# Encoder trunk on one core: rotary tables built beside the projections, vector loads on another queue, a two-part sum of squares, and a drawn order in the mixer's opening

## The chip, the cores and the metric

The kernel runs on one core of a Trainium2 chip. The metric is the device time of one execution in microseconds (us). The engines of the core run side by side: PE (TensorE, matmuls), DVE (VectorE), ACT (ScalarE), POOL (GpSimd) and SP (SyncE, here only a queue that issues transfers). Each engine takes its instructions in the order in which the program lists them; an instruction whose operand is not ready holds up everything behind it on its engine. A DMA can be issued from the queue of SP or of ACT.

## What is computed

Two layers of an encoder over 1024 tokens of width 1024. Cut to what matters here:

```python
cos, sin = rope_tables(positions)              # 1024 x 16 each
c_act = silu(c)
for l in range(2):
    mod = c_act @ w_ada[l] + b_ada[l]          # shift, scale, gate for both sub-layers
    h = rmsnorm(x, g_mix[l]) * (1 + scale_a) + shift_a
    proj = h @ w_in[l]                         # q,k,v of the neighbourhood branch, c_q, c_kv, k_rope, gates
    # latent branch: q = rmsnorm(c_q) @ w_uq; its rotary part is turned by cos, sin
    ...                                        # two attention branches, gates, merge
    x = x + gate_a * (merged @ w_out[l])
    h = rmsnorm(x, g_mlp[l]) * (1 + scale_m) + shift_m
    x = x + gate_m * (square(relu(h @ w_ff1[l])) @ w_ff2[l])
return rmsnorm(x, g_final)
```

## The kernel before

A scheduler puts the instructions of all engines into one order when the kernel is built; `keep_in_program_order` (called `pin`) keeps an instruction at its place among the pinned ones. Activations lie transposed, 128 channels by 512 tokens to a tile, two halves of the tokens (`ch` 0 and 1). Every fp32 operand of a matmul is split into a high part (a cast on ACT, L201) and a low part (a subtraction on DVE, L202), and a product is three matmuls, high by high, high by low and low by high (L208 to L210, or L459 to L461). So each operand costs ACT and DVE one instruction before PE can use it. Below, "h lo" and "wq lo" are such subtractions for the activations and the weights.

**The opening.** SP's queue issues the loads of `c`, the positions, eight rows `xrow` of x (512 KB each), seven small vectors (`vrows`, L116), and then 16 tiles `wada` of 512 KB with the adaLN weights for the first scale and the first shift. DVE first builds the rotary tables: the angles of all positions, in turns, reduced to their fraction by exact pieces (L302 to L325), from which ACT computes `sinT` and `cosT` by Sin (L350, L351) with a load of the Sin table before and of the Exp/Ln table behind. ACT squares the rows of x (L337), POOL makes of each sum a reciprocal root and a diagonal matrix `dg` (L338 to L342), and PE multiplies xrow by it into `pyT`, which transposes and scales in one step. DVE adds up the `wada` tiles with the weights `c_act`, one row each (L169, then L171): eight for the scale, eight for the shift. PE turns the sums (`pada`), DVE reduces them (`mod`), and with them the normed x becomes h.

**The projections** (`projections`, L449). Eight units of `ptok` (24 matmuls each) give `ctok`, that is c_q, c_kv and k_rope for 128 tokens each; `c_sink` copies and scales them on DVE, `cg`, `cqh` and `cql` are their transposed high and low parts. Eight units with the weights `ws` of `vws` give `vtok`. Beside these `query_rot` turns c_q into rotary queries: PE `pqr`, DVE `rot` and `qrr` (L386 to L392, which read sinT and cosT), and two units later `query_turn` transposes them (`pqrT`, L756). A further eight wada tiles are added up here for the next vector of the modulation.

**The norm before the mixer and the final ones.** `square_sum` squares each of eight channel tiles on ACT and adds it to `sums` on DVE; `rstd_first` multiplies `sums` by a matrix of ones in fp32 on PE (`pss`), which gives every partition the sum over channels; DVE takes `var` from it. This happens six times in a run: for both halves before each of the two mixers, and for both halves before layer 1's projections.

**The mixer's opening** (`mixer_norm_rest` and `mixer`). The mixer multiplies by Winograd's form of Strassen's scheme: seven products p = 1..7 for each step i, of sums of blocks of h and of the weights. In what follows (i,p) is such a product, 12 matmuls of 128x512. `norm` is a generator that, in steps between the first products, scales the second half of h and makes the sums `operand_h(p, k, ...)`; `weight_operands` makes the sums `s` of the weights. The order of the products is written out, the order of the DVE and ACT work below them is the scheduler's.

Of the kernel before, what the change touches and what calls it, by code (L numbers as in the profile page):

```python
# [18 lines left out]
P = 128  # L19
# [18 lines left out]
def hybrid_trunk(  # L38
# [89 lines left out]
    nc.sync.dma_start(pint, positions.rearrange("a (i p) -> (a i) p", p=P))  # L128
# [71 lines left out]
    def split(dst_hi, dst_lo, src, pin=lambda ins: ins):  # L200
        pin(A.copy(dst_hi, src))  # L201
        V.tensor_tensor(dst_lo, src, dst_hi.bitcast(F32), op=ALU.subtract)  # L202
# [28 lines left out]
    sums = [None, None]  # L231

    def square_sum(src, ch, n):
# [64 lines left out]
    n, chunks, magic = P, turn_chunks(), 1.5 * 2.0 ** 23  # L298
    turns, rest = (pool["ws"].tile([P, 2048], F32, tag="ws", name=s) for s in ("turns", "rest"))
    ang, parts = rest[:, 1792:1920], rest[:, 1536:1792]  # L300
    for i in range(8):
        V.tensor_scalar(ang[:, i * 16:(i + 1) * 16], invf, posT[:, i:i + 1], None, op0=ALU.mult)  # L302
    ahi = parts[:, n:]
    V.tensor_copy(ahi.bitcast(F32R), ang)
    V.tensor_tensor(parts[:, :n], ang, ahi, op=ALU.subtract)

    def frac(t):
        w = rest[:, :t.shape[1]]
        V.tensor_scalar(w, t, magic, magic, op0=ALU.add, op1=ALU.subtract)
        V.tensor_tensor(t, t, w, op=ALU.subtract)  # L310

    m = 2 * n * len(chunks)
    for i, cval in enumerate(chunks):
        V.tensor_scalar(turns[:, 2 * n * i:2 * n * (i + 1)], parts, cval, None, op0=ALU.mult)
    frac(turns[:, :m])
    frac(turns[:, :m])
    while m > n:
        half = m // n // 2 * n
        V.tensor_tensor(turns[:, :half], turns[:, :half], turns[:, m - half:m], op=ALU.add)
        frac(turns[:, :half])  # L320
        m -= half
    two_pi = 2.0 * math.pi * (1 - 2.0 ** -22)
    flat = lambda t: t[:].rearrange("p a b -> p (a b)")
    turn, quarter = turns[:, :n], turns[:, n:2 * n]
    V.tensor_scalar(quarter, turn, 0.25, None, op0=ALU.add)  # L325
    frac(quarter)
# [1219 lines left out]
```

## Time and profile before

| | |
|---|---|
| median of 3 runs | 3153.73 us (3151.32 to 3154.35) |
| the profiled execution | 3154.83 us, its span 3153.0 us |
| mean granted clock of PE | 0.988 |
| PE busy | 3033.6 us, 96% |
| DVE / ACT / POOL busy | 66% / 47% / 12% |

PE is nearly always busy, so what counts is the time in which it waits, and what it is waiting for. A busy share of the other engines is an average over stages of very different kinds. The profiled execution lies 1.10 us above the median.

### The profile page before, as it was taken

The numbers are of one execution on the slowest core, as the hardware profiler recorded it, in microseconds if no ns is written. First come the engines' busy times: TensorE is split into PE (matmuls) and PEld (weight loads), VectorE is DVE, ScalarE is ACT, GpSimd is POOL, SyncE is SP. The second block draws the span as 40 slices with busy tenths as digits, with TensorE's granted clock in tenths as the row PEclk, the third lists the DMA queues.
The fourth block names the chain that finished last, engine by engine and source line by source line (L and its number), as shares of the span: only waits on it lengthen the run. The fifth ranks groups of instructions, "written<-read, shape, count | busy, mean of one in ns | idle before, by whom it ended". The sixth has DMA issues, their size and how long they took to land. (4 is left out here: it accounts for less than half of the span.)

```text
span 3153.0 us, 43333 instructions
## 1 busy us (share of the span) xinstructions
PE 3033.6 (96%) x15104; PEld 2456.0 (78%) x15104; DVE 2069.4 (66%) x3911; ACT 1471.2 (47%) x2820; POOL 373.0 (12%) x518
## 2 busy tenths in 40 slices
PE   7999999999998999999989999999999999999998
PEld 6878886776786888888777788777777778888887
DVE  8534436767859776877774334466775697767775
ACT  6234446554127666433352444555522466663332
POOL 5111002232200000000011011123221000000000
PEclk9999999999999999999999999999999999999999
DMA  6554334214853656856334444431266255586652
GB/s 258 157 135 111 99 109 119 63 36 145 280 191 107 244 207 231 293 196 209 106 121 138 125 121 114 117 86 36 73 214 218 69 180 214 211 308 205 215 166 84
DMA packets 359540, 497.56 MB, mean 158 GB/s; under 512 B 30556, under 2 KB 238618, under 8 KB 359322
## 3 DMA queue, kind: packets, MB, share of 16 engines
q1 hardware_dynamic: 359322, 494.80, 48.9%
q8 instruction: 119, 1.95, 0.3%
q14 instruction: 99, 0.81, 0.1%
HBM read 335.41 MB, written 141.98 MB: 151 GB/s over the span
## 5 line engine op out<-in xcount | busy, mean ns | idle before, releaser
L208 PE MATMUL pd<-h,wh 128*128 128x512 f32 x768 | 307.0, 400 | 0.6 <-ACT wh L201 0.6
L210 PE MATMUL pd<-h,wh 128*128 128x512 f32 x768 | 300.7, 392 | 0.0
L209 PE MATMUL pd<-h,wh 128*128 128x512 f32 x768 | 300.1, 391 | 0.0
L208 PE MATMUL pxz<-ho,wq 128*128 128x512 f32 x672 | 259.9, 392 | 3.5 <-DVE xT L1401 3.0
L209 PE MATMUL pxz<-ho,wq 128*128 128x512 f32 x672 | 261.8, 390 | 0.5 <-DVE ho L1153 0.5
L210 PE MATMUL pxz<-ho,wq 128*128 128x512 f32 x672 | 257.0, 389 | 0.0
L201 ACT CAST wq<-s 128x512 fp32r<-128x512 f32 (+3 forms) x296 | 154.5, 541 | 125.5 <-PE pxz L210 54.2
L208 PE MATMUL px<-h,wq 128*128 128x512 f32 x512 | 202.2, 396 | 3.5 <-ACT u L1242 2.3
L1401 DVE SCALAR_TENSOR_TENSOR xT<-pxz,mod,xT 128x512 f32<-128x512 f32 x252 | 186.7, 744 | 28.4 <-PE pxz L210 28.3
L798 DVE TENSOR_REDUCE sm<-smla 128x1 f32<-128x1024 f32 x128 | 156.6, 1223 | 69.7 <-PE smla L796 63.3
L209 PE MATMUL px<-h,wq 128*128 128x512 f32 x512 | 200.2, 392 | 1.4 <-DVE h L202 1.4
L210 PE MATMUL px<-h,wq 128*128 128x512 f32 x512 | 199.6, 391 | 0.0
L801 ACT ACTIVATE pmla<-smla,sm 128x1024 f32<-128x1024 f32 x128 | 143.0, 1117 | 118.2 <-DVE sm L799 113.3
L803 POOL TENSOR_SCALAR pmla<-pmla,sm 128x1024 f32<-128x1024 f32 x128 | 144.6, 1130 | 330.4 <-DVE sm L799 153.7
L202 DVE TENSOR_TENSOR wq<-s,wq 128x512 fp32r<-128x512 f32 (+3 forms) x296 | 168.7, 582 | 6.9 <-ACT wq L201 6.9
L796 PE MATMUL smla<-st,st 128*128 128x512 f32 x512 | 170.4, 413 | 2.9 <-ACT pmla L801 2.9
L208 PEld LDWEIGHTS pd<-h,wh 128*128 128x128 f32 x768 | 144.9, 189 | 32.4 <-issue 3.4
L210 PEld LDWEIGHTS pd<-h,wh 128*128 128x128 f32 x768 | 144.6, 188 | 32.8 <-issue 1.0
L209 PEld LDWEIGHTS pd<-h,wh 128*128 128x128 f32 x768 | 145.1, 189 | 28.3
L201 ACT CAST wq<-wr 128x384 fp32r<-128x384 f32 (+3 forms) x218 | 114.7, 539 | 106.2 <-PE pxz L210 62.6
L209 PE MATMUL pyz<-h,wq 128*128 128x512 f32 x384 | 151.6, 395 | 8.0 <-DVE h L202 8.0
L208 PEld LDWEIGHTS pxz<-ho,wq 128*128 128x128 f32 x672 | 126.1, 188 | 36.3 <-issue 4.8
(281 smaller groups left out, 7344.3 us busy)
## 6 DMA issues: line engine op xcount, KB each, us to landing
hid_d<-diff SPq DMA_DIRECT2D x112, 512.0 KB
ho<-hid_d SPq DMA_DIRECT2D x112, 512.0 KB
wada<-in_w_ada_dram SPq DMA_DIRECT2D x96, 512.0 KB
wr<-in_w_ff_dram SPq DMA_DIRECT2D x64, 512.0 KB
w<-in_w_in_dram SPq DMA_DIRECT2D x56, 512.0 KB
wr<-in_w_ff_dram SPq DMA_DIRECT2D x64, 384.0 KB
ho<-hid_d SPq DMA_DIRECT2D x84, 256.0 KB
hid_d<-u SPq DMA_DIRECT2D x68, 256.0 KB
```

The costliest lines, as they stand in the source:

```text
L201: pin(A.copy(dst_hi, src))
L202: V.tensor_tensor(dst_lo, src, dst_hi.bitcast(F32), op=ALU.subtract)
L208: T.matmul(ps, wh, mh, start=first and i == 0, stop=False, **kw)
L209: T.matmul(ps, wh, ml, start=False, stop=False, **kw)
L210: T.matmul(ps, wl, mh, start=False, stop=i == n - 1, **kw)
L796: T.matmul(ps[:, cs(ch)], a[:, t], b[:, cs(ch)], start=i == 0, stop=i == 2)
L798: V.reduce_max(sm[:, 0:1], ps, axis=AX.X)
L801: A.activation(pt, ps, AF.Exp, bias=sm[:, 1:2], scale=MLA_SCALE, accum_out=sm[:, 2:3])
L803: G.tensor_scalar(pt, pt, sm[:, 3:4], 1.0, op0=ALU.mult, op1=ALU.mult)
L1401: V.scalar_tensor_tensor(x, ps, gate_m[:, nt:nt + 1], x, op0=ALU.mult, op1=ALU.add)
```

## The change

Four edits. (1) The rotary tables are no longer built ahead of the opening's adaLN sums; `rotary_tables` is called from `c_sink` with the fifth unit of `ptok` in layer 0, works in three slabs instead of two weight tiles, and pins its first eight rows and its two Sins. (2) The nine loads of vectors and positions are issued from ACT's queue instead of SP's. (3) The last of the eight squares is no longer added to `sums` on DVE; a second fp32 matmul with ones adds it on PE, in the same bank. (4) In the mixer's opening `follow` makes instructions follow others on the same engine: the scaling of tile k = 4 of the second half follows the last `operand_h(5, 3)`, and the weight sums of the work items 8 to 11 follow its DVE part.

```diff
 def load_rows(group, base):
-            nc.sync.dma_start(t[n:n + cnt, :], flat.rearrange("(r p) -> r p", p=P))
+            nc.scalar.dma_start(t[n:n + cnt, :], flat.rearrange("(r p) -> r p", p=P))
...
-    nc.sync.dma_start(pint, positions.rearrange("a (i p) -> (a i) p", p=P))
+    nc.scalar.dma_start(pint, positions.rearrange("a (i p) -> (a i) p", p=P))
...
+    def follow(ins, prev):
+        tc.add_manual_dep(ins.ins, prev.ins.name, mybir.DependencyInfo(mybir.DependencyClass.NoSync, mybir.DependencyReason.DATA),
+                          reason="order of the mixer's opening")
+        return ins
...
             sq = tmp("sq")
             A.activation(sq, src, AF.Square)
-            V.tensor_tensor(sums[ch], sums[ch], sq, op=ALU.add)
+            if n < 7:
+                V.tensor_tensor(sums[ch], sums[ch], sq, op=ALU.add)
+            else:
+                last_sq[ch] = sq
...
-        T.matmul(ps, ones, sums[ch], start=True, stop=True)
+        T.matmul(ps, ones, sums[ch], start=True, stop=False)
+        T.matmul(ps, ones, last_sq[ch], start=False, stop=True)
...
+    def rotary_tables():
+        n, chunks, magic = P, turn_chunks(), 1.5 * 2.0 ** 23
+        ta, tb, tw = (slab(s) for s in ("turns", "turns", "rest"))
...
+        pin(A.activation(flat(sinT), turn, AF.Sin, scale=two_pi))
+        pin(A.activation(flat(cosT), quarter, AF.Sin, scale=two_pi))
+        exp_ln_tables()
...
+            if i == 4 and l == 0:
+                rotary_tables()
...
+                v = V.tensor_tensor(y, y, r, op=ALU.mult)
+                a = A.activation(y, y, AF.Identity, scale=amlp[l][:, k:k + 1], bias=shift_m[:, k:k + 1])
+                if k == 4 and ch == 1:
+                    follow(a, opening[0])
+                    follow(v, opening[1])
...
-                operand_h(5, k, top[k][0])
+                opening[:] = operand_h(5, k, top[k][0])
...
+            ins = V.tensor_tensor(t, x0, x1, op=op)
+            if wait_opening[0]:
+                follow(ins, wait_opening[0])
...
+            wait_opening[0] = opening[1] if 8 <= n < 12 else None
```

What this does to the order of the engines is shown at three places. SP's queue at the start of the program, before (xrow is a row of x, vrows the small vectors, wada the adaLN weights):

```order
L132 DMA xrow_98<-in_x_dram 128x1024
L132 DMA xrow_100<-in_x_dram 128x1024
L116 DMA vrows_102<-in_b_ada_dram 96x128
L116 DMA vrows_102<-in_g_mix_dram 16x128
L116 DMA vrows_105<-in_g_mlp_dram 16x128
L116 DMA vrows_105<-in_g_final_dram 8x128
L116 DMA vrows_105<-in_b_gate_dram 32x128
L116 DMA vrows_105<-in_g_q_dram 4x128
L116 DMA vrows_105<-in_g_kv_dram 2x128
L160 DMA wada_201<-in_w_ada_dram 128x1024
L160 DMA wada_203<-in_w_ada_dram 128x1024
```

The same place on SP's queue in the change:

```order
L132 DMA xrow_98<-in_x_dram 128x1024
L132 DMA xrow_100<-in_x_dram 128x1024
L160 DMA wada_164<-in_w_ada_dram 128x1024
L160 DMA wada_166<-in_w_ada_dram 128x1024
L160 DMA wada_168<-in_w_ada_dram 128x1024
```

The loads of wada stand directly behind those of x; the two loads that stood ahead of x have gone too, and all nine now head ACT's queue, before its first table load.

DVE beside the first units of the projections, before, up to the first rotary rows (`rot`, `qrr`), which are rows 147 and 148 of DVE's order:

```order
L169 TENSOR_SCALAR ada_1563<-wada_1564,c_act 128x1024
L171 SCALAR_TENSOR_TENSOR ada_1563<-wada_1567,c_act,ada_1563 128x1024
L664 TENSOR_SCALAR cg_1062<-pcT_1058,cols 128x128 x3
L171 SCALAR_TENSOR_TENSOR ada_1563<-wada_1570,c_act,ada_1563 128x1024
L202 TENSOR_TENSOR cql_725<-cg_1062,cqh_724 128x128
L202 TENSOR_TENSOR cql_727<-cg_1062,cqh_726 128x128
L202 TENSOR_TENSOR cql_729<-cg_1062,cqh_728 128x128
L664 TENSOR_SCALAR cg_1106<-pcT_1102,cols 128x128 x3
L171 SCALAR_TENSOR_TENSOR ada_1563<-wada_1573,c_act,ada_1563 128x1024
L386 TENSOR_TENSOR rot_1125<-pqr_1117,sinT 128x128
L387 TENSOR_TENSOR qrr_1124<-pqr_1117,cosT 128x8x16
```

DVE ahead of the same rotary rows in the change, where they are rows 157 and 159 (turns and rest are the tables in the making):

```order
L171 SCALAR_TENSOR_TENSOR ada_1568<-wada_1587,c_act,ada_1568 128x1024
L321 TENSOR_SCALAR rest_804<-turns_802 128x384
L171 SCALAR_TENSOR_TENSOR ada_1568<-wada_1590,c_act,ada_1568 128x1024
L322 TENSOR_TENSOR turns_802<-turns_802,rest_804 128x384
L334 TENSOR_TENSOR turns_802<-turns_802 128x128
L321 TENSOR_SCALAR rest_804<-turns_802 128x128
L322 TENSOR_TENSOR turns_802<-turns_802,rest_804 128x128
L339 TENSOR_SCALAR turns_802<-turns_802 128x128
L402 TENSOR_TENSOR rot_1130<-pqr_1122,sinT 128x128
L322 TENSOR_TENSOR turns_802<-turns_802,rest_804 128x128
L403 TENSOR_TENSOR qrr_1129<-pqr_1122,cosT 128x8x16
```

Four of the eight wada rows (three L171 and the L169) stood ahead of the first `rot` before, and all eight do now, with the rows of the tables between them. PE's order of units is unchanged here: `pqr` for two tiles, the second unit of vtok, `pqrT` twice, `pqr`, the third unit.

DVE in the mixer's opening of layer 0, before (u<-pyz are rows on finished products, xT the scaling and the sums of h; h_8669 is the low part of the first operand of p = 5, wq_8758 that of the weights of (0,3)):

```order
L1284 TENSOR_TENSOR u_8694<-pyz_8781,u_8694 128x512
L1162 TENSOR_TENSOR s_8800<-wr_8633,s_8798 128x512
L1162 TENSOR_TENSOR s_8884<-wr_8624 128x512
L202 TENSOR_TENSOR wq_8758<-s_8756,wq_8758 128x512
L1162 TENSOR_TENSOR s_8923<-wr_8631 128x512
L1284 TENSOR_TENSOR u_8722<-pyz_8833,u_8722 128x512
L1077 TENSOR_TENSOR xT_7947<-xT_7951,xT_7947 128x512
L1077 TENSOR_TENSOR xT_7948<-xT_7952,xT_7948 128x512
L202 TENSOR_TENSOR h_8669<-xT_7947,h_8669 128x512
```

DVE around the same operand in the change (numbers of tiles are five higher):

```order
L1063 TENSOR_TENSOR xT_7959<-xT_7959,r_1505_8618 128x512
L202 TENSOR_TENSOR wq_8731<-s_8729,wq_8731 128x512
L1088 TENSOR_TENSOR xT_7952<-xT_7952 128x512
L1088 TENSOR_TENSOR xT_7953<-xT_7953 128x512
L1088 TENSOR_TENSOR xT_7954<-xT_7954 128x512
L1311 TENSOR_TENSOR u_8699<-pyz_8786,u_8699 128x512
L1088 TENSOR_TENSOR xT_7955<-xT_7955 128x512
L1311 TENSOR_TENSOR u_8727<-pyz_8838,u_8727 128x512
L1100 TENSOR_TENSOR xT_7953<-xT_7957,xT_7953 128x512
L202 TENSOR_TENSOR h_8674<-xT_7952,h_8674 128x512
```

Counted from `var`, the row behind pss, h_8669 was the 37th row of DVE and is the 27th as h_8674; the low part of the weights of (0,3), which was the 32nd, is the 46th as wq_8763. Layer 1 has the same rows in both orders, but for wq of (0,3), which was the 62nd there.

## Rows read from the trace of the kernel before

**Rows 1.** The page, busy time and share of the span by engine.
```profile
PE 3033.6 (96%) x15104; PEld 2456.0 (78%) x15104; DVE 2069.4 (66%) x3911; ACT 1471.2 (47%) x2820; POOL 373.0 (12%) x518
```
**Rows 2.** Waits of PE: line, waited for, us in all, times, longest.
```profile
PE pyT L347 <- POOL dg L342: 11.1, 5, 6.4
```
**Rows 3.** Timeline of SP's queue: start us, us, rows issued.
```profile
1.51 3.76 SPq L132 DMA_DIRECT2D xrow<-in_x_dram  x8
...
15.14 13.95 SPq L160 DMA_DIRECT2D wada<-in_w_ada_dram  x16
```
**Rows 4.** Timeline of DVE in the opening: start, us, rows, idle before.
```profile
13.71 0.62 DVE L309 TENSOR_SCALAR rest<-turns 128x768 f32<-128x768 f32 x1
14.36 0.96 DVE L310 TENSOR_TENSOR turns<-turns,rest 128x768 f32<-128x768 f32 x1
...
19.71 0.75 DVE L169 TENSOR_SCALAR ada<-wada,c_act 128x1024 f32<-128x1024 f32 x1
...
38.08 1.28 DVE L187 TENSOR_REDUCE mod<-pada 128x4 f32<-128x512 f32 x2
...
42.08 3.92 DVE L171 SCALAR_TENSOR_TENSOR ada<-wada,c_act,ada 128x1024 f32<-128x1024 f32 x3
```
**Rows 5.** Timeline of PE in the opening.
```profile
28.05 8.37 PE L347 MATMUL pyT<-dg,xrow 128*128 128x128 f32 x58 [2.15 <-POOL dg L342]
...
55.19 0.45 PE L459 MATMUL ptok<-ws,h 128*128 128x416 f32 x1
```
**Rows 6.** Timeline of POOL in the opening.
```profile
8.18 1.90 POOL L342 TENSOR_SCALAR dg<-ident,xss 128x128 f32<-128x128 f32 x1
```
**Rows 7.** Timeline of DVE beside the projections.
```profile
84.18 1.22 DVE L202 TENSOR_TENSOR ws<-w,ws 128x1024 fp32r<-128x1024 f32 x1
...
110.62 1.27 DVE L171 SCALAR_TENSOR_TENSOR ada<-wada,c_act,ada 128x1024 f32<-128x1024 f32 x1
111.82 0.28 DVE L386 TENSOR_TENSOR rot<-pqr,sinT 128x128 f32<-128x128 f32 x1
```
**Rows 8.** Timeline of PE at the first rotary queries.
```profile
117.89 0.66 PE L756 MATMUL pqrT<-ident,qrr 128*128 128x128 f32 x2 [1.87 <-DVE qrr L392]
```
**Rows 9.** Timeline of PE at three of the six sums of squares.
```profile
933.32 1.02 PE L245 MATMUL pss<-sums,ones 128*128 128x512 f32 x2
...
953.36 1.59 PE L245 MATMUL pss<-sums,ones 128*128 128x512 f32 x2 [2.65 <-DVE sums L241]
...
1598.42 1.54 PE L245 MATMUL pss<-sums,ones 128*128 128x512 f32 x2 [2.90 <-DVE sums L241]
```
**Rows 10.** Timeline of PE in the mixers' openings, layer 0 and layer 1.
```profile
978.00 0.80 PE L209 MATMUL pyz<-h,wq 128*128 128x512 f32 x1 [4.31 <-DVE h L202]
...
1001.13 0.50 PE L208 MATMUL px<-h,wq 128*128 128x512 f32 x1 [0.53 <-ACT u L1253]
...
2520.91 0.80 PE L209 MATMUL pyz<-h,wq 128*128 128x512 f32 x1 [3.71 <-DVE h L202]
...
2536.56 0.50 PE L210 MATMUL pyz<-h,wq 128*128 128x512 f32 x1 [2.05 <-DVE wq L202]
...
2545.95 0.50 PE L208 MATMUL px<-h,wq 128*128 128x512 f32 x1 [0.22 <-ACT u L1253]
```
**Rows 11.** Timeline of DVE, the row behind `pss` in both mixers' openings.
```profile
954.99 0.69 DVE L247 TENSOR_SCALAR var<-pss 128x512 f32<-128x512 f32 x1 [1.69 <-PE pss L245]
...
2498.49 0.69 DVE L247 TENSOR_SCALAR var<-pss 128x512 f32<-128x512 f32 x1 [2.03 <-PE pss L245]
```
**Rows 12.** Windows: us, then busy time (instructions) of PE, PEld, DVE, ACT, POOL, clock, DMA.
```profile
84.00:112.00 28.00, 28.00 (x148) 25.16 (x147) 20.97 (x54) 10.61 (x35) 6.08 (x13) 1.00 0.58 175
125.00:150.00 25.00, 25.00 (x130) 21.17 (x128) 8.59 (x34) 4.00 (x10) 0.00 (x0) 1.00 0.38 118
955.00:980.00 25.00, 20.19 (x79) 15.77 (x79) 25.00 (x42) 21.16 (x36) 0.00 (x0) 0.91 0.23 71
1005.00:1030.00 25.00, 23.84 (x106) 19.39 (x105) 23.20 (x40) 20.72 (x38) 0.00 (x0) 1.00 0.63 215
```

More of the change, by code (lines that the diff above doesn't have):

```diff
@@ L229, in hybrid_trunk @@
     pipe = Pipe()
-    sums = [None, None]
+    sums, last_sq = [None, None], [None, None]
     def square_sum(src, ch, n):
@@ L297, in hybrid_trunk @@
     dense_open()
[L298 to L322, printed above, removed]
+    def rotary_tables():
+        n, chunks, magic = P, turn_chunks(), 1.5 * 2.0 ** 23
+        ta, tb, tw = (slab(s) for s in ("turns", "turns", "rest"))
+        parts, ang = tw[:, 768:1024], ta[:, 896:1024]
+        for i in range(8):
+            pin(V.tensor_scalar(ang[:, i * 16:(i + 1) * 16], invf, posT[:, i:i + 1], None, op0=ALU.mult))
+        ahi = parts[:, n:]
+        V.tensor_copy(ahi.bitcast(F32R), ang)
+        V.tensor_tensor(parts[:, :n], ang, ahi, op=ALU.subtract)
+        def frac(t):
+            w = tw[:, :t.shape[1]]
+            V.tensor_scalar(w, t, magic, magic, op0=ALU.add, op1=ALU.subtract)
+            V.tensor_tensor(t, t, w, op=ALU.subtract)
+        m = n * len(chunks)
+        for t, cut in ((ta, chunks[:len(chunks) // 2]), (tb, chunks[len(chunks) // 2:])):
+            for i, cval in enumerate(cut):
+                V.tensor_scalar(t[:, 2 * n * i:2 * n * (i + 1)], parts, cval, None, op0=ALU.mult)
+            frac(t[:, :m])
+            frac(t[:, :m])
+        V.tensor_tensor(ta[:, :m], ta[:, :m], tb[:, :m], op=ALU.add)
+        frac(ta[:, :m])
+        while m > n:
+            half = m // n // 2 * n
+            V.tensor_tensor(ta[:, :half], ta[:, :half], ta[:, m - half:m], op=ALU.add)
+            frac(ta[:, :half])
+            m -= half
+        two_pi = 2.0 * math.pi * (1 - 2.0 ** -22)
+        turn, quarter = ta[:, :n], ta[:, n:2 * n]
+        V.tensor_scalar(quarter, turn, 0.25, None, op0=ALU.add)
+        frac(quarter)
+        pin(A.activation(flat(sinT), turn, AF.Sin, scale=two_pi))
+        pin(A.activation(flat(cosT), quarter, AF.Sin, scale=two_pi))
+        exp_ln_tables()
@@ L323, in hybrid_trunk @@
     flat = lambda t: t[:].rearrange("p a b -> p (a b)")
-    turn, quarter = turns[:, :n], turns[:, n:2 * n]
-    V.tensor_scalar(quarter, turn, 0.25, None, op0=ALU.add)
-    frac(quarter)
+    pin = tc.keep_in_program_order
     x_d = dram.tile([D, S], F32, name="x_d")
@@ L349, in hybrid_trunk @@
             A.copy(yT[k][:, cs(ch)], ps)
-    tc.keep_in_program_order(A.activation(flat(sinT), turn, AF.Sin, scale=two_pi))
-    tc.keep_in_program_order(A.activation(flat(cosT), quarter, AF.Sin, scale=two_pi))
-    exp_ln_tables()
-    pin = tc.keep_in_program_order
     ada_sum(acc1, first_scale, 0, pin)
@@ L1044, in scaled @@
                 y = xs[k][:, cs(ch)]
-                V.tensor_tensor(y, y, r, op=ALU.mult)
-                A.activation(y, y, AF.Identity, scale=amlp[l][:, k:k + 1], bias=shift_m[:, k:k + 1])
+                v = V.tensor_tensor(y, y, r, op=ALU.mult)
[3 more added lines that the diff above has]
+                    follow(v, opening[1])
+        opening = []
         def mixer_norm():
@@ L1101, in layer @@
         dense_close()
-        xs = mixer(l, hq, gate_m, norm)
+        xs = mixer(l, hq, gate_m, norm, opening)
         nh = [[], []]
@@ L1190, in weight_operands, with mixer @@
         return make
-    def mixer(l, hq, gate_m, norm):
+    def mixer(l, hq, gate_m, norm, opening):
         pool_open("ff", 8, side="left")
```

8 lines of the change are left out of this document (4 added, 4 removed).

## The prediction

> **What bounds the kernel now.** The page comes first: PE is busy for 3033.6 of the 3153.0 us of the span [rows 1], so no engine can give much but by ending a wait of PE or taking work from it. The waits of PE come next: the longest entry in the opening is pyT waiting 11.1 us for POOL's dg, 6.4 of it at once [rows 2]. PE's timeline there shows more idle time than that row names, because the first projection matmul starts only at 55.19 [rows 5]; it needs h, h needs the scale and the shift, and those are 16 sums of DVE. So I read DVE's timeline: it is busy with the rotary tables until 19.71, begins its first wada row there, and finishes the last three at 42.08 + 3.92 = 46.0 [rows 4]. Behind the opening, three more places matter: the first rotary queries, where PE waits 1.87 us for qrr [rows 8]; the matmul with ones [rows 9]; and the mixers' openings, where PE waits 4.31 us in layer 0, and 3.71 and 2.05 us in layer 1, for low parts from DVE [rows 10]. Around those DVE has no idle time: 42 rows in 25 us, 0.60 each [rows 12], so there an operand is as late as its rank in DVE's order.
>
> **The opening.** SP has issued x by 5.27 and its first wada only at 15.14 [rows 3], with seven small loads between. Those were issued one by one as rows of x landed, so the first wada left when the last x was in. Without them wada stands directly behind x in the queue. Two loads ahead of x go too, which starts x earlier than 1.51 [rows 3], by an estimated 0.8. A tile of 512 KB took 1.3 us in the stream: the last of the sixteen was issued at 15.14 + 13.95 = 29.1, as the eighth landed, and the first had landed by 19.71 [rows 3, 4]. The first wada then lands at 15.1 - 0.8 + 1.3 = 15.6, where DVE began on it at 19.71, and the sixteenth 15 x 1.31 later, at 35.3. DVE is free by then, since the tables (some 16 us, summed below) have left. Thirteen sums keep pace with the loads and end at 15.6 + 12 x 1.31 + 1.3 = 32.6. Then stand, in the new order, the columns, two reductions (1.28) and three small rows, some 2.2 us to 34.8, and the last three sums (3.92) end at 38.7, against 46.0: **7.3 us earlier**. What follows (ws lo, reductions, h) keeps its distances, so ptok starts at 47.9. pyT must not be in the way, because the columns stand behind it on PE: the last square of x ends about 15.6, a dg took up to 1.90 beside DVE's table rows [rows 6] and a reciprocal root as much, so the eighth is there by 20 even with DVE busy again, and PE's 58 matmuls behind it take 8.37 [rows 5], which ends at 28.4, four us before the columns are asked for. Bounds: 4.0 if only the transfers' gain comes through, and 9.5 if DVE's three last sums are let in earlier and PE's clock stays up.
>
> The Trainium skill ("DMA: Bandwidth & Descriptors", section "Issuing engines are not separate DMA queues") says that issuing from several engines saves only the time that the sequencer takes to issue. The queue's rows here show another saving, a wait between 5.27 and 15.14; by the rule alone the nine issues' own time, 3.2 us, would be gained in place of the 4.1 us by which I let the first wada land earlier, and the opening would give about 6.4.
>
> **The projections.** Here the tables come back: 16 us of rows on DVE, placed among rows that PE waits for. The order shows that they stand ahead of the first `rot`, which cannot run without sinT, and that all eight wada sums do so as well, four of them new. I add up what DVE has to do from the first ws lo, which starts at 84.18 [rows 7] when PE has delivered the fifth ptok: four ws lo at 1.13 (4.5), eight wada sums at 1.20 from start to start (9.1; the row at 110.62 is followed at 111.82), 29 short rows for ctok, cg, cql and uqr at 0.2 to 0.5 (11.2), and the table rows up to `rot`: five reductions to the fraction of 768 columns at 0.62 + 0.96 [rows 4] and a gap, 1.64 each (8.2), one sum of 768 (1.0), the angles and pieces (3.1), and the small rows at the end (4.0), 16.3 in all. Together 41.1 us, where 27.6 passed before: `rot` starts at 125.2 instead of 111.82. One load's 1.3 us comes on top if a wada is late. A dozen rows of 0.2 and the cosine on ACT lead to the second qrr, 3.3 us later, at 128.5 to 130. PE's order is the same as before: pqrT for the second tile started at 117.89 [rows 8]; the vtok unit ahead of it ends at 114.4, and PE has nothing else to run. It waits some 14 us and starts pqrT at 129.2, **11.3 us later** in the old frame. Lower bound 8 (if short rows overlap more than their pitch says), upper 13 (if every wada is late and the clock falls behind the wait). None of it comes back later: from 125 to 150 PE was busy for 25.00 of 25 us [rows 12], so the queue behind pqrT is full. Sin and its two table loads cost nothing: ACT has finished its casts by then and the next vtok waits for PE.
>
> **The two-part sum.** It takes a DVE addition off the chain and puts a second fp32 matmul on PE. In a run of matmuls pss takes 1.02 us busy, and two together hold PE for 0.9 more; at half clock the same takes 1.5 to 1.9 [rows 9]. For the first half before both mixers and before layer 1 PE does not wait for it, so the second one is pure cost, 3 x 0.87 = 2.6. For the second half before layer 1, at 1598.42, PE waits 2.90; the three sums behind the ctok copy still stand there, and the added matmul costs 0.9 to 1.9, I take 1.2. **Together +3.8.** For the mixers' second halves PE's wait of 2.65 [rows 9] falls by one DVE row, 0.6, and the added matmul takes that back: `var` moves by -0.2 to +1.3; I take +0.2 and +0.1 and carry them below.
>
> **The mixers' opening.** Count from var, V = 954.99 and 2498.49 [rows 11]. PE waits for the first low part of p = 5 (37th row). It now is the 27th, 6 us earlier, and both of those waits go [rows 10]. But a stall goes on to the next late operand. The weights of (0,3) are now the 46th row, ready at 46 x 0.60 and a little, V + 28.4. PE, which reached p = 5 at 978.00 - 4.31 = V + 18.7 and needs 24 matmuls at 0.225 for it (106 in 23.84 us [rows 12]), gets there some 3 to 4 us before, so the stall moves on with DVE's rank, not with PE. Behind it stand the first two matmuls of (2,5), whose weights ACT casts at V + 35.8, then the low part of h for (0,6), the 60th row, V + 36.9. From there 56 matmuls (12.6 us) and 0.7 us of half clock lead to the start of (0,4) at V + 50.2. Before, (0,7) started at 1001.13 and 2545.95 [rows 10]; with 24 matmuls, 5.4 us, (0,4) stood at V + 51.6 and V + 52.9. The gains are 1.3 and 2.7, less the shift of V: -1.1 and -2.6, **together -3.7**, with +1 if half clock follows the new waits and -6 if it follows none.
>
> **Sum.** -7.3 + 11.3 + 3.8 - 3.7 = +4.1 on the execution of 3154.83: 3158.9. That execution lies 1.1 above the median, which makes 3157.8 beside the median 3153.73. The change is then +0.13%; 0.2%, or 6.3 us, is about what a measurement of this kernel can tell from no change.
>
> **Rivals.** (a) *The tables fit in.* If their rows go into DVE's gaps and `rot` is not late, the opening's gain stands: 3153.7 - 7.3 + 0 + 3.8 - 3.7 = 3146.5, faster. It decides for faster as long as pqrT is less than 0.9 us late. For it: DVE was busy only 20.97 of the 28 us from 84 to 112 [rows 12]. Against it: 16.3 + 4.8 us of added rows do not fit into 7 us of gaps, and the order lets no row pass. Chance 0.19, with the case that the mixers give their whole bound. (b) *The opening gives less, and the projections take all.* If pyT, behind which the columns stand on PE, still holds DVE, the opening yields only the 4.0 us of the transfers, and with qrr at 130.5 the sum is -4 + 12.5 + 3.8 - 3.7 = +8.6, 3162.3. It decides for slower from an opening of less than 5 us on, or a `rot` later than 127.5. (c) *The drawn order does nothing or harm*: the stall only moves to wq of (0,3) and half clock follows it; then -3.7 becomes +1 and the time is 3162.5 with the rest as summed. It and (b) share a chance of 0.31.
>
> **How the numbers follow.** My forecast, within 6.3 us of the old median, has a chance of 0.5; (a) 0.19, faster; (b) with (c) 0.31, slower. The range: opening -9.5 to -4, projections 8 to 13, sums 3.3 to 5, mixers -6 to +1. All at their best they give -4.2, all at their worst +15, that is 3149.5 and 3168.7 from the median. They will not all lie at one end, but (a) reaches lower: I set 3146 to 3165.
>
> **What would show it.** Right: DVE's first wada row at about 15.6 and ptok at about 48; a wait of PE at pqrT of some 14 us for qrr; two L254/L255 matmuls at each sum, PE no longer waiting at the first low part of p = 5 but at wq of (0,3). Wrong: ptok after 51; the wait at pqrT under 6 us; or a PE wait of over 5 us anywhere in the mixers' openings.

## The result, and the profile after

| | before | after |
|---|---|---|
| median, run side by side | 3153.46 us (3151.32 to 3154.35) | 3174.74 us (3169.36 to 3176.45) |
| ratio, 95% interval | | 1.0066 (1.0048 to 1.0083) |
| span of the profiled execution | 3153.0 us | 3172.0 us |

The change is slower by 0.66%, some 21 us, and the time lies above the range. The two profiled executions differ by 19.0 us; the account below is made on them. PE has no more work than before, within 2 us [rows 1]; the rest is waiting.

```profile
PE 3035.5 (96%) x15116; PEld 2456.1 (77%) x15116; DVE 2070.1 (65%) x3909; ACT 1472.4 (46%) x2820; POOL 377.4 (12%) x518
```

A milestone table comes first: when the same instruction starts in both, so that the difference between two lines is what one stretch lost.

| starts (us) | before | after | later by |
|---|---|---|---|
| first square of x (ACT) | 5.23 | 10.82 | 5.6 |
| first ptok (PE) | 55.19 | 56.57 | 1.4 |
| first pcT (PE) | 71.14 | 75.59 | 4.5 |
| first pqr (PE) | 107.42 | 113.54 | 6.1 |
| third pqr, behind pqrT (PE) | 118.20 | 137.41 | 19.2 |
| second `var` of layer 0's mixer (DVE) | 954.99 | 974.13 | 19.1 |
| second `var` of layer 1's mixer (DVE) | 2498.49 | 2519.19 | 20.7 |
| end | 3153.0 | 3172.0 | 19.0 |

So 6.1 us are lost up to the first rotary queries and 13.1 us at the turn of these queries. One pair of profiles has its scatter, and the kernels of the experiments repeat these stretches. Four with the opening of before (before, only_square, only_follow, only_mixer) start ptok at 54.5 to 55.9 and pqr at 106.7 to 107.8; five with that of after (after, u_square, u_follow, double_frac, tables_loads) at 54.4 to 56.9 and 111.0 to 114.2. So the 1.4 us at ptok lie within the scatter, and the loss at pqr does not. All that is behind them, with the two-part sums and the drawn orders in it, comes to -0.3 us in this pair (18.95 less 19.21).

**The opening.** The queues of ACT and SP (start, us, what was issued, how many), then ACT's first work; answers to [rows 3]:

```profile
2.04 0.44 ACTq L116 DMA_DIRECT2D vrows<-in_g_mix_dram  x1
4.57 0.32 ACTq L116 DMA_DIRECT2D vrows<-in_g_mlp_dram  x1
...
9.14 0.24 ACTq L116 DMA_DIRECT2D vrows<-in_g_kv_dram  x1
9.41 1.28 ACT L149 ACT_TABLE_LOAD   x1 [9.41 <-DMA vrows<-in_g_final_dram]
...
0.72 8.36 SPq L132 DMA_DIRECT2D xrow<-in_x_dram  x8
10.07 14.51 SPq L160 DMA_DIRECT2D wada<-in_w_ada_dram  x16
```

SP's first wada leaves at 10.07, not 15.14, as wanted. But the nine loads wait in ACT's queue as they did in SP's: from 2.04 on, gaps of up to 2.1 us stand between issues of about 0.3 us. ACT is an engine with work, and all of that work stands behind its issues: the table load ends its idle time at 9.41, the first square starts at 10.82. The eight issues of x now take 8.36 us, where they took 3.76 [rows 3].

POOL's `dg` at the start, in the middle and at the end, an answer to [rows 6]; then DVE, an answer to [rows 4]; then PE, to [rows 5]:

```profile
14.36 0.37 POOL L362 TENSOR_SCALAR dg<-ident,xss 128x128 f32<-128x128 f32 x1
...
30.96 1.42 POOL L362 TENSOR_SCALAR dg<-ident,xss 128x128 f32<-128x128 f32 x1
...
32.99 0.37 POOL L362 TENSOR_SCALAR dg<-ident,xss 128x128 f32<-128x128 f32 x1
```

```profile
15.40 0.75 DVE L169 TENSOR_SCALAR ada<-wada,c_act 128x1024 f32<-128x1024 f32 x1 [4.29 <-DMA wada<-in_w_ada_dram]
...
26.89 5.25 DVE L171 SCALAR_TENSOR_TENSOR ada<-wada,c_act,ada 128x1024 f32<-128x1024 f32 x4 [0.30 <-DMA wada<-in_w_ada_dram]
42.63 0.42 DVE L124 COPY cols<-pcols 128x112 f32<-128x112 f32 x2 [10.49 <-PE pcols L123]
...
45.23 3.92 DVE L171 SCALAR_TENSOR_TENSOR ada<-wada,c_act,ada 128x1024 f32<-128x1024 f32 x3
```

```profile
33.42 9.08 PE L367 MATMUL pyT<-dg,xrow 128*128 128x128 f32 x58 [0.19 <-POOL dg L362]
42.33 0.46 PE L123 MATMUL pcols<-ident,vrows 112*128 112x112 f32 x2
...
56.57 0.46 PE L475 MATMUL ptok<-ws,h 128*128 128x416 f32 x1 [0.83 <-ACT h L201]
...
75.59 0.66 PE L678 MATMUL pcT<-ident,ctok 128*128 128x128 f32 x2 [5.12 <-DVE ctok L499]
```

DVE begins the sums at 15.40 and has 13 done by 32.1. Then it stands for 10.49 us, because `pcols` lies behind `pyT` on PE, `pyT` behind the eighth `dg` at 32.99, and the `dg` rows run beside DVE's sums: 1.42 us each where they take 0.37 beside an idle DVE. The Trainium skill ("GPSIMD Engine Reference", section "Specifications") has GpSimd share its SBUF interfaces with VectorE, and contention where DVE reads two SBUF inputs, as L171 does; these rows agree. The last three sums end at 49.15, not at 38.7.

The last row shows a loss behind ptok: PE is through its first three ptok units and waits 5.12 us for `ctok`. Before, it waited 0.50 us there:

```profile
71.14 0.44 PE L660 MATMUL pcT<-ident,ctok 128*128 128x128 f32 x2 [0.50 <-DVE ctok L483]
```

Windows of the stretch in after, columns as in [rows 12], and then one of before:

```profile
62.00:69.00 7.00, 7.00 (x39) 6.92 (x38) 5.62 (x8) 3.27 (x6) 7.00 (x6) 1.00 0.95 378
69.00:76.00 7.00, 1.88 (x11) 1.55 (x9) 4.95 (x9) 3.69 (x15) 4.00 (x9) 0.75 0.00 2
76.00:84.00 8.00, 8.00 (x38) 7.73 (x37) 3.78 (x14) 1.81 (x8) 2.32 (x7) 0.79 0.05 16
...
76.00:84.00 8.00, 8.00 (x47) 7.83 (x46) 5.15 (x20) 4.07 (x17) 2.41 (x7) 1.00 0.17 51
```

Behind the wait the granted clock is at the lower level (1.2 GHz) for part of the next 8 us, 0.79 in the mean, where it was 1.00 before. These 8 us at 0.79 are worth 1.7 us, and by 1.7 us the way from the first pcT to the first pqr is longer (37.95 for 36.28).

**The projections.** DVE ahead of the first `rot`, an answer to [rows 7], and PE, to [rows 8]:

```profile
127.31 1.28 DVE L171 SCALAR_TENSOR_TENSOR ada<-wada,c_act,ada 128x1024 f32<-128x1024 f32 x1
128.50 0.35 DVE L321 TENSOR_SCALAR rest<-turns 128x384 f32<-128x384 f32 x1
129.39 1.28 DVE L171 SCALAR_TENSOR_TENSOR ada<-wada,c_act,ada 128x1024 f32<-128x1024 f32 x1 [0.53 <-DMA wada<-in_w_ada_dram]
...
133.40 0.28 DVE L402 TENSOR_TENSOR rot<-pqr,sinT 128x128 f32<-128x128 f32 x1
```

```profile
136.60 1.16 PE L774 MATMUL pqrT<-ident,qrr 128*128 128x128 f32 x4 [12.86 <-DVE qrr L408]
```

**Sums and mixers' openings.** PE at the second half before layer 0's mixer and before layer 1's projections (answers to [rows 9]), and the waits in the mixers' openings (to [rows 10]):

```profile
972.11 1.13 PE L254 MATMUL pss<-sums,ones 128*128 128x512 f32 x2 [2.05 <-DVE sums L248]
973.07 1.02 PE L255 MATMUL pss<-sq,ones 128*128 128x512 f32 x2
...
998.92 0.50 PE L214 MATMUL pyz<-h,wq 128*128 128x512 f32 x1 [2.40 <-ACT wq L201]
1002.81 0.79 PE L216 MATMUL pyz<-h,wq 128*128 128x512 f32 x1 [2.15 <-DVE wq L202]
...
1618.00 1.40 PE L254 MATMUL pss<-sums,ones 128*128 128x512 f32 x2 [2.81 <-DVE sums L248]
1619.20 1.91 PE L255 MATMUL pss<-sq,ones 128*128 128x512 f32 x2
...
2536.85 0.50 PE L215 MATMUL pyz<-h,wq 128*128 128x512 f32 x1 [0.90 <-DVE h L202]
2544.52 0.50 PE L214 MATMUL pyz<-h,wq 128*128 128x512 f32 x1 [2.39 <-ACT wq L201]
2548.41 0.79 PE L216 MATMUL pyz<-h,wq 128*128 128x512 f32 x1 [2.15 <-DVE wq L202]
```

The wait of 4.31 us at the first low part is gone in layer 0 and 0.90 us in layer 1, and in each layer two waits, of 2.4 and 2.15 us, stand behind it at the weights.

### The profile page after: what moved, and what is told of

It reads as the page before. It is cut to its first block, busy times and chain, and to the rows that moved or that the text cites. A ratio compares the mean times of both kernels' runs of the same rounds, so it can differ in the third digit from the quotient of the medians.

```text
span 3172.0 us, 43368 instructions
## 1 busy us (share of the span) xinstructions
PE 3035.5 (96%) x15116; PEld 2456.1 (77%) x15116; DVE 2070.1 (65%) x3909; ACT 1472.4 (46%) x2820; POOL 377.4 (12%) x518
## 5 line engine op out<-in xcount | busy, mean ns | idle before, releaser
L214 PE MATMUL pyz<-h,wq 128*128 128x512 f32 x384 | 151.2, 394 | 5.8 <-ACT wq L201 5.7
L216 PE MATMUL pyz<-h,wq 128*128 128x512 f32 x384 | 151.5, 395 | 4.3 <-DVE wq L202 4.3
```

Of the source, the lines that this page charges most:

```text
L214: T.matmul(ps, wh, mh, start=first and i == 0, stop=False, **kw)
L216: T.matmul(ps, wl, mh, start=False, stop=i == n - 1, **kw)
```

## The experiments

The theories: **A**, the opening loses because ACT stands behind its issues; **P**, the projections lose what DVE has to do ahead of `rot`; **I**, an earlier ptok is lost again because of PE's interleaved order of the first three ptok units. Their rivals put the loss into the sums, the drawn order, or drift. Every ratio is to runs of the kernel before on the same chip in the same session, since its own median went from 3152.3 to 3157.1 between the sessions, which were on different chips; the last column is the ratio's distance from 1, times 3153.5 us.

| kernel | ratio (95%) | us |
|---|---|---|
| after | 1.0066 (1.0048 to 1.0083) | +20.8 |
| u_queue: after, loads on SP | 1.0075 (1.0060 to 1.0090) | +23.7 |
| u_tables: after, tables first | 1.0021 (1.0007 to 1.0034) | +6.6 |
| u_square: after, one matmul | 1.0049 (1.0032 to 1.0066) | +15.5 |
| u_follow: after, no drawn order | 1.0067 (1.0048 to 1.0087) | +21.1 |
| double_frac: after, more table rows | 1.0079 (1.0062 to 1.0096) | +24.9 |
| only_tables | 1.0044 (1.0031 to 1.0057) | +13.9 |
| tables_loads | 1.0048 (1.0035 to 1.0060) | +15.1 |
| only_square | 1.0013 (1.0004 to 1.0022) | +4.1 |
| only_follow | 0.9984 (0.9975 to 0.9992) | -5.0 |
| only_mixer: square and follow | 1.0023 (1.0014 to 1.0032) | +7.3 |
| vec_pool: after, loads behind dg | 1.0047 (1.0031 to 1.0063) | +14.8 |
| vec_pool_early | 1.0037 (1.0024 to 1.0051) | +11.7 |
| vec_pool_before | 0.9995 (0.9985 to 1.0005) | -1.6 |
| vec_pool_third | 1.0006 (0.9997 to 1.0016) | +1.9 |
| vec_split | 1.0002 (0.9993 to 1.0011) | +0.6 |
| split_before | 0.9998 (0.9989 to 1.0007) | -0.6 |
| vec_split_follow | 0.9988 (0.9978 to 0.9999) | -3.8 |

**u_queue.**

```diff
-            nc.scalar.dma_start(t[n:n + cnt, :], flat.rearrange("(r p) -> r p", p=P))
+            nc.sync.dma_start(t[n:n + cnt, :], flat.rearrange("(r p) -> r p", p=P))
```

> The change with the nine small loads back on SP's queue; the other three edits stay. Theory A (ACT's queue): in the changed kernel ACT cannot square x before its nine issues are through, at 9.4, and so the diagonals of POOL are made beside DVE's wada sums and pyT ends at 42.5. With the loads on SP the squares begin at 5.2, the eighth dg is there by 19, pyT ends by 29, the first wada lands at 19 to 20, the last opening sum ends at 42 to 43 instead of 49.1, and the first projection matmul starts at 49 to 51 instead of 56.57. The wait at pqrT stays (12 to 15 us). Total 3161 to 3166. Theory B (POOL beside DVE alone, whatever ACT does): pyT still ends after 36, the first projection matmul starts at 54 or later, total 3170 or more.

The last `dg` and the first ptok in its timelines of POOL and PE:

```profile
16.91 0.37 POOL L362 TENSOR_SCALAR dg<-ident,xss 128x128 f32<-128x128 f32 x1
```

```profile
50.90 0.46 PE L475 MATMUL ptok<-ws,h 128*128 128x416 f32 x1 [0.83 <-ACT h L201]
...
71.14 0.66 PE L678 MATMUL pcT<-ident,ctok 128*128 128x128 f32 x2 [5.65 <-DVE ctok L499]
```

A holds in its own place: all eight `dg` take 0.37 us, since DVE has nothing to do before 18.40, and ptok starts 5.7 us earlier than after. The total did not follow. By the first pqr the 5.7 are 3.1, by the third 2.8, at the second `var` of layer 0's mixer 0.7, and the profile ends 4.8 us behind that of after. All along DVE's and ACT's orders behind the opening are those of after, so two profiles with the same order drift by several us; one place is a `pf` before layer 1's projections, where PE waits 3.71 us in this profile and 2.24 in that of after. What sets this drift is not shown, and the loads' share of the total is not settled by this run.

**u_tables, double_frac.** The first puts the tables back ahead of the opening's sums; the second takes four fractions where two do, which leaves the result as it is.

```diff
...
-            if i == 4 and l == 0:
-                rotary_tables()
...
```

```diff
-            frac(t[:, :m])
-            frac(t[:, :m])
+            for _ in range(4):
+                frac(t[:, :m])
```

> The change with the rotary tables back in the opening; the other three edits stay. Theory P (the tables stand before the rotary queries and PE waits for them): the wait of 12.9 us at pqrT falls under 4 us and the stretch from the first ws lo to the second pqr is 34 us again instead of 47. Theory A adds that the opening is still late, because ACT's squares begin at 10.8 and POOL then works beside table rows and wada sums: the first projection matmul at 56 to 60. Total 3156 to 3162. Rival (the opening and not the projections holds the loss): total stays above 3168.

> The change with the reduction to the fraction of 768 columns done four times instead of twice on both halves (a repeated reduction changes nothing in the result); 8 more rows, 6.3 us of DVE, ahead of the first rot. Theory P (the sum of DVE's rows ahead of rot sets the wait): the wait at pqrT grows from 12.9 to 19 us, the total from 3174.7 to 3181. Rival (the wait is set by something else, a late wada or ACT): the wait stays within 2 us.

PE at pqrT in u_tables, then in double_frac:

```profile
121.87 0.44 PE L766 MATMUL pqrT<-ident,qrr 128*128 128x128 f32 x2 [1.24 <-DVE qrr L402]
124.17 0.66 PE L766 MATMUL pqrT<-ident,qrr 128*128 128x128 f32 x2 [1.86 <-DVE qrr L402]
```

```profile
140.00 1.16 PE L774 MATMUL pqrT<-ident,qrr 128*128 128x128 f32 x4 [18.85 <-DVE qrr L408]
```

Without the tables pqr and the third pqr are late by the same 6.1 and 6.3 us, so the 13 us are gone, and the ratio falls by 14 us. With 6.3 us of rows more, the wait grows by 6.0 us, and so does DVE's way from its first ws lo to `rot` (43.1 us in after, 49.1 here). The opening of that profile came 2.6 us earlier at pqr, so pqrT stands 3.4 us later on the clock and the total 4.1 us, less than its interval. P holds, from both sides.

**u_square, u_follow, only_square, only_follow, only_mixer.** These take out, or do alone, the second matmul and the two uses of `follow`.

```diff
-            if n < 7:
-                V.tensor_tensor(sums[ch], sums[ch], sq, op=ALU.add)
-            else:
-                last_sq[ch] = sq
+            V.tensor_tensor(sums[ch], sums[ch], sq, op=ALU.add)
...
```

```diff
-                if k == 4 and ch == 1:
-                    follow(a, opening[0])
-                    follow(v, opening[1])
...
-            if wait_opening[0]:
-                follow(ins, wait_opening[0])
```

> The change with the last square added on DVE again and one matmul with ones; the other three edits stay. By the prediction's term the second matmul costs about 0.9 us each where PE does not wait for it and 1.2 before layer 1: the kernel becomes 3 to 4 us faster (about 3171). Rival: the second matmul is paid for by the addition that it takes off DVE's chain, and the time stays within 1 us of 3174.7. The profile decides by the time between the rows on both sides of the sums.

> The change without the drawn order in the mixer's opening; the other three edits stay. By the prediction's term the order is worth 1.3 us in layer 0 and 2.7 in layer 1 counted from the row var: without it the kernel becomes 3 to 4 us slower (about 3178), and PE waits over 3 us at the first low part of p = 5 in both layers again. Rival: the stall has only moved to the weights of (0,3) and (2,5), and the time stays within 1 us of 3174.7.

> The kernel before with the two-part sum alone: eight squares as before, the last one added by a second fp32 matmul instead of DVE, no drawn order. Direct cost alone, as the traces have it (from the first to the second pss +0.26 before either mixer, +0.8 before layer 1, and as much again behind the second halves): 1.5 to 4 us, 3154 to 3156.5. Rival (the edit also takes away a better order of the copies in layer 1's first ptok units, worth some 5 us, which the order alone gives): 3157 to 3160, with PE's wait at pcT in layer 1 still 3.4 us where the drawn order alone has 1.5.

> The kernel before with the drawn order in the mixer's opening alone. Forecast's step (it is worth 1.3 us in layer 0 and 2.7 in layer 1): PE's wait at the first low part of p = 5 (4.31 and 3.71 us) goes, a smaller one stands at the weights of (0,3), and the total is 3149 to 3151. Rival (the stall only moves, half clock follows it): 3152.5 to 3155, the stretch from var to (0,7) as long as before within 0.5 us.

> The kernel before with the two-part sum and the drawn order, tables and loads as before. Forecast's sum for both: +3.8 - 3.7, 3153.8. If the added matmuls cost nothing where PE waits anyway, 3150; if they cost what they hold PE in each of the six places and the drawn order gives nothing, 3159 (6 x 0.9 = 5.4). In the three places where PE does not wait for pss it holds PE for 0.8 to 1.0 us more.

The two-part sum alone costs 4.1 us (1.3 to 6.9), on top of all else 5.3 (1.0066 less 1.0049, whose intervals overlap). Its direct part is in the traces: from the first to the second pss stands 0.26 us more before either mixer, 0.81 more before layer 1, in every kernel with two matmuls and in none with one. The drawn order alone gives 5.0 us; on top of the three other edits it gives nothing (1.0067 without, 1.0066 with). The two together, alone, should then give -0.9, and they cost 7.3.

Part of that lies where neither edit is. The scheduler also put DVE's copies in layer 1's first ptok units into another order. PE's first pcT there, in only_follow, only_square and only_mixer:

```profile
1615.50 0.44 PE L666 MATMUL pcT<-ident,ctok 128*128 128x128 f32 x2 [1.53 <-DVE ctok L489]
```

```profile
1623.16 0.44 PE L670 MATMUL pcT<-ident,ctok 128*128 128x128 f32 x2 [0.94 <-DVE ctok L493]
```

```profile
1627.12 0.69 PE L670 MATMUL pcT<-ident,ctok 128*128 128x128 f32 x2 [3.45 <-DVE ctok L493]
```

The wait is 3.44 us in the kernel before and 3.45 in after. From the second pss there to the sixteenth vtok the kernel before took 102.7 us, only_follow 95.3, only_mixer 98.5, after 100.9. So 7.4 of the 8.8 us by which only_follow's profile is shorter lie there, not in the mixers. But vec_pool_before took 95.2 us there too and is no faster in total, so this order does not decide the time alone. Four pairs of kernels differ by the drawn order alone. Where the sum has one matmul it pays, 5.0 us (only_follow) and 4.4 (vec_split_follow less vec_split); beside the two-part sum it costs 3.2 (only_mixer less only_square) or gives 0.3 (after less u_follow). Only the first of these is clear of the intervals, and whether and why the order pays only without the two-part sum stays open. The rival of only_square's expectation (a loss of the better order) is refuted by its 0.94, though its median of 3160.3 lies in that rival's range: the kernel before stood at 3157.1 in that session.

**only_tables, tables_loads.** Edit 1 alone; edits 1 and 2.

```diff
...
+            if i == 4 and l == 0:
+                rotary_tables()
...
```

```diff
-    nc.sync.dma_start(pint, positions.rearrange("a (i p) -> (a i) p", p=P))
+    nc.scalar.dma_start(pint, positions.rearrange("a (i p) -> (a i) p", p=P))
```

> The kernel before with the tables beside the projections alone: loads on SP's queue as before, one matmul with ones, no drawn order. If the loss lies where DVE's rows ahead of the first rotary row stand: ptok 4 us earlier than before (50.9, as with the vectors back on SP's queue), the first rotary queries 3 us later, PE waits 10 to 13 us at pqrT, the total is 3168 to 3171. Rival (much of the loss sits in the edits of the sums): 3160 to 3164.

> The change without the two-part sum and without the drawn order: tables beside the projections and the nine loads on ACT's queue. If ACT's queue costs what it costs at the first rotary queries (3 us more than the tables alone): 3168 to 3171, against 3166.4 for the tables alone. Rival (the loss at ptok is given back later, as the loads moved back to SP's queue gained nothing in the total): 3165 to 3167.

The tables alone cost 13.9 us, though ptok starts 5.3 us earlier: the first pqr is 1.6 us later, the third 13.8. The loads add 4.0 us at the first pqr in the profiles and 1.2 us (less than their intervals) in the total. The sum by single edits is then 13.9 + 1.2 for tables and loads, 5.3 for the sums, 0 for the drawn order: 20.4 of the 20.8 measured, with 4 to 6 us of uncertainty in each ratio. That the sum closes is near to given, since the last two are taken with the other edits in place; it does not show that the edits add up in another order.

**vec_pool, vec_pool_before, vec_pool_third.** To get the wada loads early without ACT, seven vector loads are issued from POOL's queue behind its last `dg`, in the change and in the kernel before; the third also lets PE's third ptok unit follow the second.

```diff
-            nc.scalar.dma_start(t[n:n + cnt, :], flat.rearrange("(r p) -> r p", p=P))
+            ins = queue.dma_start(t[n:n + cnt, :], flat.rearrange("(r p) -> r p", p=P))
...
+    ta, na_ = load_rows(rows_a, 0, nc.gpsimd)
+    tb, nb_ = load_rows(rows_b, 128, nc.gpsimd)
```

```diff
+                    if k == 0 and i == 2 and l == 0 and width == 416:
+                        follow(first, unit_end[1])
```

> The change with c and the positions on SP ahead of x, wada directly behind x, and the seven other vectors issued from POOL behind its last dg, so that neither ACT's squares nor the stream of wada wait for them. If theory A (ACT's queue) is the whole error of the opening's term, the first projection matmul starts at 47 to 49, as predicted for the change, in place of 56.57. If POOL beside DVE's wada sums is a bound of its own, it starts after 52. The first three units of ptok are still interleaved as in the change, and PE waits 5 to 6 us for the first pcT; the first pqr comes 0 to 2 us later than before and the total is 3165 to 3170.

> The kernel before, with only the loads moved as in vec_pool; tables, sums and mixer as before. The tables hold DVE until 19.7, then 16 sums run without waiting for loads: the first projection matmul at 50 to 52 instead of 55.19. The scheduler here interleaves the first three units of ptok as in the change. Theory I (the third unit's matmuls used to cover the turn-round of the first two, and are now spent earlier): PE waits 4 to 6 us for the first pcT and the first pqr is no earlier than 107; total 3152 to 3155. Rival (the wait at pcT belongs to the tables' edit): no wait over 1 us there, total 3148 to 3151.

> vec_pool_before with one more dependency: in layer 0 the third unit of ptok follows the second on PE. Theory I: the wait for the first pcT falls under 1 us, the first pqr starts at 102 to 104 instead of 107.42, and the total is 3148 to 3151. Rival (the turn-round is late for another reason, POOL or ACT): the wait at pcT stays over 3 us and the total does not fall below that of vec_pool_before.

ptok comes 5.5, 4.2 and 2.2 us earlier than before, and the first pqr 0.7, 1.5 and 1.2 us later. In vec_pool, where ACT has no loads to issue and the squares start at 5.14, the eighth `dg` ends at 18.9, `pyT` at 29.0 and the last sum at 39.9, and ptok starts at 49.6:

```profile
17.74 1.18 POOL L362 TENSOR_SCALAR dg<-ident,xss 128x128 f32<-128x128 f32 x1
```

So A is nearly the whole error up to ptok. In the total vec_pool is 6.0 us faster than after, but their intervals overlap. PE at the first pcT, in vec_pool_before and then vec_pool_third:

```profile
70.11 0.66 PE L664 MATMUL pcT<-ident,ctok 128*128 128x128 f32 x2 [5.17 <-DVE ctok L487]
```

```profile
70.97 0.66 PE L674 MATMUL pcT<-ident,ctok 128*128 128x128 f32 x2 [3.71 <-DVE ctok L497]
```

I falls as the main cause: with PE's units in their old order the wait is 3.71 us, not under 1. What pcT follows is POOL. `mod` releases 12 scalings of yT on POOL, one train, here of before and of after; then ACT's last cast of h in after:

```profile
49.44 18.31 POOL L271 TENSOR_SCALAR yT<-yT,amix,mod 128x512 f32<-128x512 f32 x12 [21.45 <-DVE mod L189]
```

```profile
52.60 18.37 POOL L281 TENSOR_SCALAR yT<-yT,amix,mod 128x512 f32<-128x512 f32 x12 [19.24 <-DVE mod L189]
```

```profile
71.01 0.62 ACT L201 CAST h<-yT 128x512 fp32r<-128x512 f32 x1 [0.56 <-POOL yT L281]
```

In after the train ends at 70.97, ACT's cast of its last row follows at once, and behind it stand the low part, the last matmuls of the three units, the copies of `ctok` and pcT, which starts 4.62 us after the train. In all 16 kernels with 12 such rows pcT starts 3.4 to 3.7 us behind the train's end (six, before among them) or 4.6 (the ten others), while ptok starts anywhere from 49.6 to 61.6. PE's order is worth some 1.1 us of that distance (4.6 in vec_pool_before, 3.5 in vec_pool_third), and the train sets the rest.

**vec_split, split_before, vec_split_follow.** So the train is shortened: 8 rows on POOL, 8 on DVE; in vec_pool_before, in the kernel before, and in vec_pool_before with the drawn order.

```diff
-            modulate(h[ch][k], y, amix[0][:, k:k + 1], mods[0][:, k:k + 1], V if ch == 0 and k % 2 else G)
+            modulate(h[ch][k], y, amix[0][:, k:k + 1], mods[0][:, k:k + 1], V if k % 2 else G)
```

> The kernel before with the vectors issued behind POOL's last dg, and 8 instead of 12 of the 16 scalings of yT on POOL (the other four on DVE). In all kernels so far the first pcT starts 3.4 to 4.6 us after POOL's last yT row, whatever ptok does. If POOL's train of yT rows is the floor: it ends at about 59.5 instead of 65.5, PE's wait at pcT falls from 5.2 us to under 1, the first rotary queries come 1.5 to 4 us earlier than in the kernel before, the total is 3148 to 3151. Rival (another thing holds pcT): the wait stays over 3 us, and the total at 3153.

> The kernel before with that split of the yT rows alone. PE waited only 0.5 us at pcT there, since ptok itself is late: no gain at pcT, and four more rows of 0.67 us stand on DVE ahead of the third and fourth weight slab, so ptok comes 0 to 2.5 us later: 3153 to 3156. Rival (POOL's rows hold PE inside the ptok units too): first pqr earlier by over 1 us, 3150 to 3152.

> vec_split with the drawn order in the mixer's opening. If the two gains add up (drawn order alone 0.9984): 3144 to 3147. If they don't, as the drawn order added nothing to the other edits: 3147 to 3151.

In vec_split POOL's train, then PE, then the window 56 to 64:

```profile
49.63 10.73 POOL L271 TENSOR_SCALAR yT<-yT,amix,mod 128x512 f32<-128x512 f32 x8 [17.45 <-ACT xT L372]
```

```profile
53.66 0.46 PE L463 MATMUL ptok<-ws,h 128*128 128x416 f32 x1 [0.83 <-ACT h L201]
...
57.38 0.46 PE L465 MATMUL ptok<-ws,h 128*128 128x416 f32 x1 [1.29 <-DVE h L202]
72.71 0.41 PE L664 MATMUL pcT<-ident,ctok 128*128 128x128 f32 x2 [1.03 <-DVE ctok L487]
```

```profile
56.00:64.00 8.00, 6.71 (x28) 6.43 (x28) 8.00 (x12) 7.15 (x14) 4.36 (x2) 0.79 1.03 415
```

The train ends at 60.4, pcT starts 12.3 us behind it and no longer follows it, and the wait at pcT falls from 5.17 to 1.03 us; so the train was what pcT waited for. But the rows taken from POOL fill DVE (8.00 of 8 us): ptok comes 2.6 us later than in vec_pool_before, PE waits inside its units for low parts of h, and pqr starts at the same 108.9. The stretch behind `mod` is bound by DVE and POOL together, and no gain of the opening passed it in these runs. The drawn order beside it (-3.8 us) does not beat the drawn order alone: only_follow has the lowest ratio of all these kernels, and is faster than both before and after.

**vec_pool_early.** vec_pool with the tables called for with the first ptok unit.

```diff
-            if i == 4 and l == 0:
+            if i == 0 and l == 0:
                 rotary_tables()
```

> The change with the vectors behind POOL's last dg, and the tables called for with the first unit of ptok instead of the fifth, so that only five of the eight wada rows stand ahead of the first rot, and the table rows lie between 52 and 112 us, where DVE has some 12 + 3 us idle. If the loss is the amount of DVE's rows that still stand ahead of rot when pqr ends: PE's wait at pqrT falls from 11.7 us to 3 to 6, and the total from 3170 to 3161 to 3165. Rival (DVE's rows there delay ctok and ws lo instead, so the loss only moves ahead): the wait falls, the first ws lo and pqr are 6 us or more later than with the fifth unit, and the total stays at 3168 to 3172.

```profile
124.70 1.16 PE L778 MATMUL pqrT<-ident,qrr 128*128 128x128 f32 x4 [8.61 <-DVE qrr L412]
```

The wait falls from 11.72 to 8.61 us, less than expected, and ws lo and pqr are not later, so the rival falls; the total is 3.1 us lower, no more than the intervals are wide. Placing the tables earlier takes back a quarter of the wait.

## Why the prediction was wrong, step by step

**The opening** (-7.3) is the step that failed; measured +1.4 at ptok and +6.1 at the first pqr. Its first half was right: the first wada row started at 15.40, forecast 15.6. Wrong was "the last square of x ends about 15.6 ... the eighth is there by 20 ... which ends at 28.4, four us before the columns are asked for". The squares end at 19.2, the eighth `dg` at 33.4, `pyT` at 42.5, ten us after. The step counted nine issues on ACT as free; they hold ACT till 9.4, and that pushes the `dg` rows beside DVE's sums, where they take 1.42 us. With ACT free (vec_pool) the step's times nearly come: the last sum ends at 39.9 for 38.7, ptok starts at 49.6 for 47.9. Rival (b) named `pyT` as the danger and priced it at a gain of 4 where it was a loss.

The sum also carried the 7.3 us on from ptok as they were: it has no term for the way from ptok to the first pqr. That was 52.2 us before and 57.0 after; u_queue, vec_pool and vec_pool_before show that even a real gain at ptok is gone there, and the trains on POOL, with vec_split, what holds it. In vec_pool the opening is nearly as forecast and pqr is still 0.7 us late. By these profiles, then, some 8 of the 13.4 us by which the opening is off at pqr are the missing term, and some 5.4 ACT's issues.

**The projections** (+11.3): the mechanism and nearly the size, 13.1 us. The term was 1.8 too small: DVE's way from the first ws lo to `rot` took 43.1 us where 41.1 were added up. PE's wait was 12.86 us where some 14 were said, and a wait of 2.78 us for `cg` at the unit ahead and the lower clock behind pqrT (granted 0.62 from 137 to 142 us) come on top. "PE has nothing else to run" and "none of it comes back" hold: 13.1 here is 13 to 14 us in the totals of u_tables and only_tables. Rival (a) fell, as its wait under 6 us did.

**The two-part sum** (+3.8): 4.1 alone and 5.3 on top, which agree with it within their intervals.

**The mixers' opening** (-3.7): the waits moved as forecast, from the first low part to wq of (0,3), and none is over 5 us. At the same matmul some 60 us behind `var` the pair of profiles has gained 1.2 us in layer 0 and 2.0 in layer 1, near the 1.3 and 2.7 of the forecast; but 113 us behind `var` only 0.2 and 0.9 are left, with a wait of 0.71 us for `u` on the way that the kernel before does not have, and the totals with and without the order are the same. The step looked no further than (0,4); from there on "the stall only moves" (rival (c)) is near the truth. The -5.0 us that it brings alone is the forecast's size, by a cause that its profile puts mostly elsewhere.

On the profiled pair the sum closes: the opening up to pqr was 13.4 worse than said (6.1 and 7.3), the projections 1.8 worse, the rest 0.4 better (-0.3, not +0.1). These are 14.8, and with the 4.1 of the forecast 18.9 of the 19.0.

## What to carry to other kernels

Here a load was not free on a queue whose engine had work behind it: before moving one, list that engine's first instructions and what they feed. A gain at one instruction is a gain of the kernel only if nothing on the way is released by something else; look from the moved instruction to the next place where PE waits, and name which engine's train ends last there. And where a scheduler orders everything, measure each edit alone and all but one: their effects here (-5.0 and +4.1) did not add up (+7.3).

## What the runs showed of the hardware

Nine DMA issues of 0.2 to 0.6 us each held ACT until 9.4 us where eight large loads were issued from SP's queue at the same time, and these took 8.36 us to issue in place of the 3.76 of [rows 3]. In the six kernels with the small loads on ACT's queue the eight took 8.0 to 8.7 us, in the thirteen without 3.8 to 3.9. The Trainium skill ("DMA: Bandwidth & Descriptors", section "Issuing engines are not separate DMA queues") says that loads of all queues interleave on the same engines; these rows fit that, and show what it can do to an engine that issues. POOL's `dg` of 128x128 took 0.37 us beside an idle DVE and 1.42 beside L171's sums.
